# Band attention of a hybrid layer: projections handed out piece by piece between a head's steps, and fixed places for the values

## The chip, the cores and the metric

One core of a Trainium2 chip runs the whole kernel. The metric is the device time of one execution in microseconds (us). The profile is that of one execution; it reports times from the start of its span.

## The reference

The kernel computes one layer of an encoder on a sequence of 1024 frames with 1024 channels, in float32. A normalised and modulated input goes through one combined projection. Its columns feed two branches. Branch A is a gated DeltaNet with 8 heads. Branch B is band attention, and it is the part that the change is about: 16 heads of 64 channels, chunks of 64 frames, each chunk attending to itself and to the 8 chunks before it.

```python
def chunk_band_attention(q, k, v, rel_bias):
    ...
    bias = rel_bias.astype(jnp.float32)[:, idx]
    key_chunk = jnp.arange(band) // CHUNK
    scale = dh ** -0.5
    ...
```

For each head the scores are q·k times 0.125 plus a bias that depends on the distance; a softmax over the band follows, and then the product with the values. Each branch's output is projected to 1024 channels, both are multiplied with sigmoid gates and added, and a last projection, a residual, a layer norm and a feed-forward part follow.

## The kernel before

**Numbers in three parts.** Every large product is made from operands split in a high and a low part of type fp32r: high·high, high·low and low·high are summed in one PSUM bank. So a projection of 128 columns for 1024 frames takes 2 halves of 8 blocks of the inner dimension times 3 products, 48 matmuls of 128x512. `load_split` (L185) loads a block from DRAM and `split` makes its parts, the high one by ACT (L177) and the low one by DVE or POOL (L180).

**The band stage** (L870 to L1014) works in 8 pairs of heads. For a pair p it needs a block of queries (column block p) and one of keys (column block 8 + p), made by `qk_proj` and the code behind it, and values. The values come for four heads at once, from `v_proj` (L890 to L907): one group g serves pairs 2g and 2g + 1, and is 8 tiles of frames times 24 matmuls of 128x256, so 192 matmuls a group and 4 groups. Its results lie in four buffers, `vts[q][o]`, with q the pair and o the half of the frames.

**One head** (`attention`, L910 to L981) is four steps of 256 queries each; head 0 has six smaller ones. The chain of a step is:

- PE makes the scores `ps` (L933); DVE adds the bias and takes the minimum of the negated scores (L936, into `sb`, which lies in the places G and FT);
- ACT takes the exponential (L941), DVE the reciprocal of the sum (L943), POOL scales (L944);
- PE transposes in 128x128 pieces into `pp` (L959); ACT makes the high part `ph` (L962), DVE the low part `pl` (L963);
- PE multiplies with the values into `po` (L974); ACT and DVE add the two halves of the result (L979, L980) into `ob`.

A head takes 24 `ps` matmuls, 30 transposes and 36 `po` matmuls on PE; head 0 takes 52 `po`.

**Blocks made ahead.** Some blocks of queries and keys are not made beside their pair but earlier, and go through DRAM (`qk_d`): those in `EP` are made during the DeltaNet stage, those in `LP` by `late_qk_block` (L782) behind head 0. Numbers under 8 are queries, those from 8 on are keys. `qk_proj` then loads such a block into a staging buffer `raw` instead of multiplying. Before the change EP is (4, 12) and LP is (2, 14). For the two blocks of keys that come this way, half of the low parts `kl` are made by POOL (L1004), the others, and all for keys that come from PSUM, by DVE.

**After the attention** comes branch A's projection (L1020 to L1085): the eight blocks of `oa_d` are loaded and split into the place of the projections' input (`hh`, `hl`), so they can be split only when the last projection of queries or keys has read it. Then for j = 0 to 7 there are two halves of 24 matmuls `pbr` (L1047). Each half loads its gates from `gates_d` into a buffer `ma[j]` (L1051), and DVE multiplies gates and PSUM (L1053). The ring of banks for it has two entries, so a half can begin only when the half two before it has been multiplied with its gates.

**Places.** SBUF is a list of named places of 4 KB a partition. A buffer in a place that is still read waits for its last reader. Before the change the values are a ring over T0, T1, T2, T3, B5, B6 and are taken by four, so that group 3 lies in T0 to T3. The gates of branch A lie in `MA`:

```python
MA = (_E1[5], _E1[6], _E0[1], _E0[3], _E0[5], "GT", "SA", "SB")
```

Here `_E1[5]` is B5, `_E1[6]` is B6, and `_E0[i]` is Ai. In PSUM the projections have banks 0 and 1 (ring "qkv"), the scores 5, 6 and 2, the transposes 3 and 4, `po` bank 7, and branch A again 0 and 1.

**What sets the order.** The order on each engine is fixed when the program is built. The framework goes through the instructions by a priority that follows the order of the program text, and issues one when its operands and its buffers are there in its own plan; so work of a later line can come between the steps of an earlier one. On the chip, each engine then takes its instructions in that order and waits in it.

Of the kernel before, what the change touches and what calls it, by code (L numbers as in the profile page):

```python
# [2 lines left out]

# [41 lines left out]
PTR = 0  # L45
G0 = 1
GA = (3, 2, 2, 2, 3, 2, 2, 99)
EP = (4,12)
OL = (1,3,5)
EPP = 1  # L50
POM = 1
# [6 lines left out]
MS = 6  # L58
PWM = ()
PWL = 0  # L60
LP = (2,14)
TS = (0,1,2)
PL = (0,1,2,3)
XM = (0,2,4,6,7)
# [6 lines left out]
_T, _E0, _E1 = ([f"{n}{i}" for i in range(m)] for n, m in (("T", 4), ("A", 7), ("B", 7)))  # L71


def _at(group, step_, n, first=0):
# [24 lines left out]
    "v": (*_T, _E1[5], _E1[6]), "qs": (_E0[0], _E0[1], "GT"), "kh": (_E0[2], _E0[3], "SA"),  # L99
# [54 lines left out]
def hybrid_layer(  # L154
# [7 lines left out]
    PE, DVE, ACT, POOL, SP = nc.tensor, nc.vector, nc.scalar, nc.gpsimd, nc.sync  # L162
# [9 lines left out]
    def f(ap):  # L172
        return ap.bitcast(F32)
# [18 lines left out]
    w_ada2, w_in2 = w_ada[0], w_in[0]  # L192
# [37 lines left out]
    hh = hpool.tile([P, NK, S], F32R, tag="hh", name="hh")  # L230
# [638 lines left out]


    def qk_proj(c0, p):
        if (c0 - Q0) // P + p in EP + LP:
            raw = W.tile([P, S], F32, tag="raw", bufs=RB, name=nm("raw"))
            SP.dma_start(raw, qk_d[(c0 - Q0) // P + p])
            for n in range(2):
                yield slice(512 * n, 512 * n + 512), raw[:, 512 * n:512 * n + 512]
            return
        w = wblock(kview(w_in2, c0 + p * P, P), NK)
        halves = []
        for n in range(2):  # L880
            ps = pbank(nm("pqk"), "qkv")
            for k in range(NK):
                for a, r in ((w[0], hh), (w[0], hl), (w[1], hh)):
                    PE.matmul(ps, a[:, k, :], r[:, k, 512 * n:512 * n + 512],  # L884
                              start=(k == 0 and a is w[0] and r is hh),
                              stop=(k == NK - 1 and a is w[1]))
            yield slice(512 * n, 512 * n + 512), ps

    def v_proj(g):
        w = [wblock(w_in2[4 * P * i:4 * P * i + 4 * P,  # L890
                          Q0 + 2 * D + 256 * g:Q0 + 2 * D + 256 * g + 256].rearrange(
                              "(k p) n -> p k n", p=P), 4) for i in range(2)]
        vts = [[ring("v", [P, 4, 2, P], F32R) for _ in range(2)] for _ in range(2)]
        for t in range(NT):
            ps = pbank(nm("pv"), "qkv")
            for k in range(NK):
                wh, wl = w[k // 4]
                for r, a in ((hh, wh), (hh, wl), (hl, wh)):
                    PE.matmul(ps[:, 0:256], r[:, k, t * P:t * P + P], a[:, k % 4, :],  # L899
                              start=(k == 0 and r is hh and a is wh),  # L900
                              stop=(k == NK - 1 and r is hl))
            for q in range(2):
                dst = vts[q][t // 4][:, t % 4]
                src = ps[:, P * q:P * q + P].rearrange("p (e d) -> p e d", e=2)
                ACT.copy(dst[:, :, 0:64], src)
                DVE.tensor_tensor(dst[:, :, 64:P], src, f(dst[:, :, 0:64]), ALU.subtract)
        return vts  # L907


    def attention(h, qs_, khh, kll, vt_, ob):  # L910
        e = h % 2
# [7 lines left out]
        for ts in ((0, 1), (2, 3), (4,), (5,), (6,), (7,)) if z else ((0, 1), (2, 3), (4, 5), (6, 7)):  # L919
# [45 lines left out]
            for ji, j in enumerate(js):  # L965
# [6 lines left out]
                for pi in ((0, 1), (1, 0))[ji == len(js) - 1 and POM]:  # L972
# [6 lines left out]
            ACT.copy(tmp[a0:a0 + 64, :], po[b0:b0 + 64, 0:n])  # L979
            DVE.tensor_tensor(ob[a0:a0 + 64, P * t0:P * t0 + n], po[a0:a0 + 64, 0:n],  # L980
                              tmp[a0:a0 + 64, :], ALU.add)  # L981

    group("GA", "G", 4096)
    group("FA", "FT", 1024)
    group("X", _E1[4], 1024, F32R)
    vts = None
    for p in range(HB // 2):
        if p % 2 == 0:
            vts = v_proj(p // 2)
        qh = [ring("qs", [P, S], F32R) for _ in range(2)]  # L990
        kh_ = [ring("kh", [P, S], F32R) for _ in range(2)]
        kl_ = [ring("kl", [P, S], F32R) for _ in range(2)]
        for sl, ps in qk_proj(Q0, p):
            for e in range(2):
                a, b = (0, 64) if e == 0 else (64, 0)
                ACT.activation(qh[e][a:a + 64, sl], ps[a:a + 64, :], AF.Copy, scale=0.125)
                DVE.scalar_tensor_tensor(qh[e][b:b + 64, sl], ps[a:a + 64, :], 0.125,
                                         f(qh[e][a:a + 64, sl]), ALU.mult, ALU.subtract)
        for sl, ps in qk_proj(Q0 + D, p):
            for e in range(2):  # L1000
                E = slice(64 * e, 64 * e + 64)
                for d_ in (64 * e, 64 - 64 * e):
                    ACT.copy(kh_[e][d_:d_ + 64, sl], ps[E, :])
                    (POOL if p + NK in EP + LP and (EPP == 2 or EPP == 1 and d_ == 64 * e) else DVE).tensor_tensor(  # L1004
                        kl_[e][d_:d_ + 64, sl], ps[E, :], f(kh_[e][E, sl]), ALU.subtract)
# [636 lines left out]
```

## Time and profile before

| | us |
|---|---|
| median of 3 runs | 2214.96 |
| lowest and highest | 2212.79, 2216.69 |
| the profiled execution | 2214.56 |
| its span in the profile | 2212.5 |
| PE busy in the span | 2121.1 |
| DVE busy | 1551.0 |
| ACT busy | 1038.3 |
| POOL busy | 583.9 |

The profile gives, for each engine, busy time in stretches of the span ("windows"), in groups by source line, and the time that it waited with what ended the wait. PE is TensorE's stream of matmuls, PEld its loads of weights, which lie beside it; DVE is VectorE, ACT ScalarE, POOL GpSimd, and SP the engine that issues most DMAs. A matmul counts as busy while it is in the pipeline, so a busy PE can still be slower than PE at its best: how many matmuls of which size it got through in a stretch says more than its busy share. The column PEclk is the clock that TensorE was granted, 1.00 being full.

The band stage's matmuls lie between 840 and 1345 us of the span, beside the end of the DeltaNet stage in front and the first of branch A's products behind.

### The profile page before, as it was taken

What the parts mean: (1) busy time and instruction counts of PE and PEld (TensorE: products, weight loads), DVE (VectorE), ACT (ScalarE), POOL (GpSimd) and SP (SyncE); (2) the same over time, 40 slices, a digit from 0 to 9 for tenths busy, and PEclk for the clock granted to TensorE, in tenths of its full rate; (3) what the DMA queues carried; (4) which work ended last, traced back from release to release, by engine and by line L of the source; (5) the groups of instructions that cost most, each with busy time, mean ns of one, the idle gap of its engine ahead of it and who ended that gap; (6) DMA issues with size and microseconds to landing.
All of it is one profiled execution on the core that took longest, in us unless ns stands there. A gap on an engine that the chain in (4) does not pass through costs nothing.

```text
span 2212.5 us, 31630 instructions
## 1 busy us (share of the span) xinstructions
PE 2121.1 (96%) x11469; PEld 1773.4 (80%) x11469; DVE 1551.0 (70%) x3228; ACT 1038.3 (47%) x2216; POOL 583.9 (26%) x544
## 2 busy tenths in 40 slices
PE   6998999999999999999999899999899999999997
PEld 5787777888878787798989788888688888887876
DVE  8467475866767754567776653556998888889897
ACT  4645243434434334466675642235544444446453
POOL 4323222332223322223442422424011000000023
PEclk9999999999999999999999999999999999999999
DMA  9232323334232412211121424342243222263222
GB/s 287 76 106 80 101 89 110 103 94 119 75 112 75 143 35 97 70 51 51 61 66 61 149 93 136 105 152 87 67 155 102 85 83 81 76 218 134 96 94 87
DMA packets 228414, 224.67 MB, mean 102 GB/s; under 512 B 27482, under 2 KB 184595, under 8 KB 228259
## 3 DMA queue, kind: packets, MB, share of 16 engines
q1 hardware_dynamic: 217939, 218.96, 31.1%
q10 hardware_dynamic: 10320, 3.70, 0.7%
q8 instruction: 90, 1.47, 0.3%
q14 instruction: 65, 0.53, 0.1%
HBM read 180.63 MB, written 48.28 MB: 103 GB/s over the span
## 4 chain that ended last, share of the span: by engine, by line
PE 44%; DVE 5%; issue 1%; POOL 1%; ACT 1%; DMA 0%; DVEq 0%; SPq 0%; ACTq 0%; POOLq 0%
PE pup L1193 18%; PE pbr L1047 8%; PE pdn L1497 5%; PE pwo L1109 4%; PE pqk L884 2%; PE pv L899 2%; PE po L974 2%; PE pp L959 1%; PE ps L933 1%; DVE hl L180 1%; DVE hh L1585 1%; DVE hh L1511 0%; ACT hh L1580 0%; POOL hh L1555 0%; DMA raw<-in_w_branch_a_dram 0%
## 5 line engine op out<-in xcount | busy, mean ns | idle before, releaser
L180 POOL TENSOR_TENSOR wl<-raw,wh 128x1024 fp32r<-128x1024 f32 x88 | 211.1, 2401 | 307.1 <-ACT wh L177 298.2
L1193 PE MATMUL pup<-hh,wop 128*128 128x512 f32 x704 | 226.0, 392 | 1.9 <-DVE wop L180 1.0
L1193 PE MATMUL pup<-t,wop 128*128 128x512 f32 x792 | 189.8, 393 | 1.8 <-ACT t L177 1.8
L1193 PEld LDWEIGHTS pup<-t,wop 128*128 128x128 f32 x792 | 149.1, 188 | 35.5 <-ACT t L177 2.2
L177 ACT CAST wh<-raw 128x1024 fp32r<-128x1024 f32 x88 | 92.4, 1051 | 152.4 <-DMA raw<-in_w_in_dram 56.4
L1193 PEld LDWEIGHTS pup<-hh,wop 128*128 128x128 f32 x704 | 132.5, 188 | 31.4 <-DVE wop L180 1.5
L284 PE MATMUL pqkv<-hh,wh 128*128 128x512 f32 x352 | 142.8, 406 | 0.2 <-ACT GT L798 0.2
L1234 POOL TENSOR_TENSOR cc<-cc,G 128x512 f32<-128x512 f32 x22 | 41.0, 1864 | 379.5 <-DVE G L1216 325.4
L284 PE MATMUL pqkv<-hl,wh 128*128 128x512 f32 x352 | 139.9, 398 | 0.0
L284 PE MATMUL pqkv<-hh,wl 128*128 128x512 f32 x352 | 138.9, 396 | 0.0
L1193 PE MATMUL pup<-hl,wop 128*128 128x512 f32 x352 | 138.0, 392 | 0.4 <-DVE hl L180 0.4
L663 DVE TENSOR_TENSOR FT<-FT,G 128x16 f32<-128x16 f32 (+30 forms) x248 | 117.7, 475 | 16.5 <-POOL G L608 9.4
L944 POOL TENSOR_SCALAR G<-G,FT 128x640 f32<-128x640 f32 (+4 forms) x103 | 69.9, 681 | 191.3 <-DVE FT L943 169.6
L177 ACT CAST wop<-wr 128x512 fp32r<-128x512 f32 x110 | 66.5, 620 | 112.8 <-DVE wr L1179 64.5
L284 PE MATMUL pgt<-hh,wl 128*128 128x512 f32 x240 | 94.9, 396 | 0.8 <-POOL wl L180 0.8
L284 PE MATMUL pgt<-hl,wh 128*128 128x512 f32 x240 | 95.0, 396 | 0.0
L284 PE MATMUL pgt<-hh,wh 128*128 128x512 f32 x240 | 95.0, 396 | 0.0
L180 DVE TENSOR_TENSOR wop<-wr,wop 128x512 fp32r<-128x512 f32 x110 | 79.7, 730 | 19.1 <-ACT wop L177 18.6
L1497 PE MATMUL pdn<-hl 128*128 128x512 f32 x360 | 85.6, 391 | 2.3 <-ACT pdn L1492 1.5
L963 DVE TENSOR_TENSOR pl<-pp,ph 128x512 fp32r<-128x512 f32 (+2 forms) x116 | 72.5, 635 | 17.3 <-ACT ph L962 16.6
L1497 PEld LDWEIGHTS pdn<-hl 128*128 128x128 f32 x360 | 67.3, 188 | 17.8 <-ACT pdn L1492 1.9
L941 ACT ACTIVATE G<-G,FT 128x640 f32<-128x640 f32 (+4 forms) x103 | 71.6, 696 | 19.2 <-DVE FT L936 17.1
(457 smaller groups left out, 6113.4 us busy)
## 6 DMA issues: line engine op xcount, KB each, us to landing
raw<-in_w_in_dram SPq DMA_DIRECT2D x72, 512.0 KB
wr<-in_w_up_dram SPq DMA_DIRECT2D x44, 512.0 KB
raw<-in_w_ada_dram SPq DMA_DIRECT2D x32, 512.0 KB
dr<-g_d SPq DMA_DIRECT2D x18, 512.0 KB
dr<-in_w_down_dram SPq DMA_DIRECT2D x18, 512.0 KB
wa<-in_w_ada_dram SPq DMA_DIRECT2D x32, 256.0 KB
gates_d<-GT SPq DMA_DIRECT2D x32, 256.0 KB
g_d<-G SPq DMA_DIRECT2D x14, 512.0 KB
```

The lines of the kernel that those rows point to most:

```text
L177: ACT.copy(h, src)
L180: return le.tensor_tensor(l, src, f(h), ALU.subtract).ins
L284: PE.matmul(ps, a[:, k, :], r[k][:, 512 * n:512 * n + 512], start=(k == 0 and a is wh and r is rh), stop=(k == NK - 1 and a is wl))
L663: DVE.tensor_tensor(pr[:, :, 0:i + 1], ft[:, :, 0:i + 1], fa[:, i:i + 1, 0:i + 1].to_broadcast([P, 8, i + 1]), ALU.mult)
L884: PE.matmul(ps, a[:, k, :], r[:, k, 512 * n:512 * n + 512], start=(k == 0 and a is w[0] and r is hh), stop=(k == NK - 1 and a is w[1]))
L941: ACT.activation(sb[:, 0:n], sb[:, 0:n], AF.Exp, bias=mx[:, nb - 1:nb], scale=-1.0, accum_out=mx[:, 2:3])
L944: POOL.tensor_scalar(sb[:, 0:n], sb[:, 0:n], mx[:, 3:4], 0.0, ALU.mult, ALU.add)
L963: DVE.tensor_tensor(pl[:, B, :], pp, f(ph[:, B, :]), ALU.subtract)
L1047: PE.matmul(ps, a[:, k, :], r[k][:, N], start=(k == 0 and a is w[0] and r is rh), stop=(k == NK - 1 and a is w[1]))
L1109: PE.matmul(ps[n], a[:, t, k, :], wo[k][b][:, 512 * n:512 * n + 512], start=(k == 0 and a is mh and b == 0), stop=(k == NK - 1 and a is ml))
L1193: PE.matmul(ps, a[:, u, k, :], b[v][k], start=(new and k == 0 and u == 0 and v == 0), stop=(k == 3 and u == 1), skip_group_check=not new)
L1497: PE.matmul(sets[s_][i], a[:, u, i * P:i * P + P], b[:, v, :], start=(new and not seed and j == 0 and u == 0 and v == 0), stop=(j == len(q ...
```

## The change

It has four parts.

- **Pieces.** `attention`, `v_proj`, `late_qk_block` and the new `qk_pair` become generators that stop (`yield`) after a step, a tile of values, or half a block. `weave` runs one step of a head, then n pieces of other work, and what is left of it behind the last step.
- **What is beside what.** Beside each odd head lie the queries and keys of the next pair. Beside the even heads of pairs 0 to 6 lie, in this order: the two late blocks, value group 1 (two pieces a step), the halves of group 2, the halves of group 3, and late block 7. A half of group 2 or 3 is one half of the frames, so each half loads the group's weights again (`again`).
- **Blocks made ahead** are now queries only: EP is (4, 6), LP is (2, 5), and LQ adds block 7 beside head 12. Their number goes from 4 to 5. All low parts of keys are made by DVE.
- **Places of the values** are fixed by a table VS, by group, pair and half of the frames. The rows stand for groups 0 to 3. Group 3 lies in B6, T2 for pair 6 and T1, B5 for pair 7.

```diff
-EP = (4,12)
+EP = (4, 6)
-LP = (2,14)
+LP = (2, 5)
+LQ = {6: (7,)}
...
+VS = ((("T0", "T1"), ("T2", "T3")), (("B5", "T0"), ("B6", "T1")),
+      (("T2", "B5"), ("T3", "T0")), (("B6", "T2"), ("T1", "B5")))
...
     def attention(h, qs_, khh, kll, vt_, ob):
...
+            yield
...
-                    (POOL if p + NK in EP + LP and (EPP == 2 or EPP == 1 and d_ == 64 * e) else DVE).tensor_tensor(
-                        kl_[e][d_:d_ + 64, sl], ps[E, :], f(kh_[e][E, sl]), ALU.subtract)
+                    DVE.tensor_tensor(kl_[e][d_:d_ + 64, sl], ps[E, :], f(kh_[e][E, sl]), ALU.subtract)
+            yield
+
+    def weave(att, other, n):
+
+        for _ in att:
+            for _ in range(n):
+                next(other, None)
+        for _ in other:
+            pass
+
+    vg = [v_proj(g, g > 1) for g in range(HB // 4)]
+    for _ in chain(vg[0], qk_pair(0)):
+        pass
+    beside = {0: (chain(*map(late_qk_block, LP)), 1), 1: (vg[1], 2), 2: (islice(vg[2], 4), 1), 3: (vg[2], 1),
+              4: (islice(vg[3], 4), 1), 5: (vg[3], 1), **{p: (chain(*map(late_qk_block, i)), 1) for p, i in LQ.items()}}
     for p in range(HB // 2):
-        if p % 2 == 0:
-            vts = v_proj(p // 2)
...
         ob = ring("ob", [P, S])
         for e in range(2):
-            attention(2 * p + e, qh[e], kh_[e], kl_[e], vts[p % 2], ob)
-            if p == 0 and e == 0:
-                for q in LP:
-                    late_qk_block(q)
+            att = attention(2 * p + e, qk[p][0][e], qk[p][1][e], qk[p][2][e], vts[p // 2][p % 2], ob)
+            weave(att, *((qk_pair(p + 1) if p + 1 < HB // 2 else iter(()), 1) if e else beside.get(p, (iter(()), 1))))
```

The built orders of before and after are the same up to the first score of the band stage. They differ from there through branch A's products. Three places are shown.

On SP, near the end of the attention, before: the gates of branch A's first two blocks (`ma_12405` is j = 0, `ma_12406` is j = 1) among the loads of `oa_d`.

```order
L185 DMA raw_12433<-oa_d 128x1024 [waits DMAHW0_49,Pool_49]
L1051 DMA ma_12405<-gates_d 128x512 [waits PE_49]
L1051 DMA ma_12405<-gates_d 128x512
L1051 DMA ma_12406<-gates_d 128x512 [waits DMAHW2_49,PE_49]
L1051 DMA ma_12406<-gates_d 128x512 [waits DMAHW3_49]
L1012 DMA ob_d<-ob_10789 128x1024 [waits DMAHW4_49,DVE_49]
```

These gates stand ahead of the store of pair 5's output (the last row), so before heads 12 to 15 are done.

On SP at the corresponding place after (line 1077 is the old 1051): `ma_12436` is j = 0, and the last row is the store of the last pair's output.

```order
L1077 DMA ma_12443<-gates_d 128x512 [waits DMAHW3_49]
L1077 DMA ma_12443<-gates_d 128x512 [waits DMAHW4_49]
L1291 DMA B_1608_12433<-mod_d 16x128 [waits DMAHW5_49,PE_49]
L1077 DMA ma_12436<-gates_d 128x512 [waits DMAHW6_49,PE_49]
L1077 DMA ma_12436<-gates_d 128x512 [waits DMAHW7_49]
L190 DMA raw_12916<-ob_d 128x1024 [waits DMAHW0_49,DVE_49]
L1038 DMA ob_d<-ob_12054 128x1024 [waits DMAHW1_49,DVE_49]
```

The gates of j = 0 have moved from ahead of pair 5's store to the last rows before pair 7's. Place B5 holds the second half of pair 7's values, and the gates wait there for PE.

On PE, the end of the last head, before: `pbr_12790` belongs to branch A's j = 5.

```order
L1047 MATMUL pbr_12790<-hl,wh_12757 128x512
L1047 MATMUL pbr_12790<-hh,wl_12758 128x512
L1047 MATMUL pbr_12790<-hh,wh_12757 128x512
L974 MATMUL po_12385<-B_852_7310,v_11181 128x256 [waits Activation_49]
L1047 MATMUL pbr_12790<-hl,wh_12757 128x512
L1047 MATMUL pbr_12790<-hh,wl_12758 128x512
L974 MATMUL po_12385<-B_852_7310,v_11181 64x256 [waits DVE_49]
```

On PE at the same place after: `pbr_12554` belongs to j = 1, and line 1073 is the old 1047.

```order
L983 MATMUL po_12416<-ph_12395,v_10381 128x128
L983 MATMUL po_12416<-pl_12396,v_10381 64x128
L983 MATMUL po_12416<-pl_12396,v_10977 64x128
L983 MATMUL po_12416<-ph_12395,v_10977 128x128
L1073 MATMUL pbr_12554<-hh,wh_12548 128x512 [waits DVE_49]
L1073 MATMUL pbr_12554<-hl,wh_12548 128x512
L1073 MATMUL pbr_12554<-hh,wl_12549 128x512
```

Before, branch products stand between the rows of the last head, and five blocks of j and part of the sixth lie ahead of its end. After, the last head's rows stand alone, and j = 1 begins behind them. Counted over the whole order, from the last matmul of a query or key projection up to the last `po`: before 60 `ps`, 120 `po` and 270 `pbr`; after 76 `ps`, 144 `po` and 48 `pbr`. Those 48 are both halves of j = 0, and behind the last of them stand 46 `ps`, 104 `po` and 76 transposes with no other matmul among them.

On ACT, where pair 6's keys come in, before: `kh_11417` is made from the block that came through DRAM (`raw`).

```order
L962 CAST ph_10504<-pp_10513 128x384
L1003 CAST kh_11417<-raw_11485 64x512 x4
L1003 CAST kh_10650<-pqk_10756 64x512
L979 COPY G_7308<-po_10483 64x256
L941 ACTIVATE G_7308,FT_7309<-G_7308,FT_7309 128x640
```

After, the same pair's keys come from PSUM (`pqk`), line 1016 being the old 1003:

```order
L950 ACTIVATE G_7308,FT_7309<-G_7308,FT_7309 128x512
L1016 CAST kh_11284<-pqk_11402 64x512
L950 ACTIVATE G_7308,FT_7309<-G_7308,FT_7309 128x640
L1016 CAST kh_11284<-pqk_11402 64x512
L1016 CAST kh_11285<-pqk_11402 64x512 x2
```

The four copies stood in one row of four; they are now spread among the exponentials.

More of the change, by code (lines that the diff above doesn't have):

```diff
@@ L2 @@
 from contextlib import ExitStack, contextmanager, nullcontext
+from itertools import chain, islice
 import concourse.bass as bass
@@ L97 @@
        for i, n in enumerate(("egl", "kss", "rk", "bk", "bkk", "nbe", "eq", "so", "ro"))},
-    "v": (*_T, _E1[5], _E1[6]), "qs": (_E0[0], _E0[1], "GT"), "kh": (_E0[2], _E0[3], "SA"),
+    "qs": (_E0[0], _E0[1], "GT"), "kh": (_E0[2], _E0[3], "SA"),
     "kl": (_E0[4], _E0[5], "SB"), "ob": (_E0[6],), "ph": (_E1[0], _E1[2]), "pl": (_E1[1], _E1[3]), "ph0": ("GT",), "pl0": ("SB",),
@@ L871, in qk_proj @@
     def qk_proj(c0, p):
-        if (c0 - Q0) // P + p in EP + LP:
+        if (c0 - Q0) // P + p in EP + LP + sum(LQ.values(), ()):
             raw = W.tile([P, S], F32, tag="raw", bufs=RB, name=nm("raw"))
@@ L887, in qk_proj, with v_proj @@
             yield slice(512 * n, 512 * n + 512), ps
[L889 to L901, printed above, removed]
-            for q in range(2):
[L903 to L907, printed above, removed]
+    def v_proj(g, again):
+        for o in range(2):
+            if o == 0 or again:
+                w = [wblock(w_in2[4 * P * i:4 * P * i + 4 * P,
+                                  Q0 + 2 * D + 256 * g:Q0 + 2 * D + 256 * g + 256].rearrange(
+                                      "(k p) n -> p k n", p=P), 4) for i in range(2)]
+            for q in range(2):
+                vts[g][q].append(place(VS[g][q][o], [P, 4, 2, P], F32R, "v"))
+            for t in range(4 * o, 4 * o + 4):
+                ps = pbank(nm("pv"), "qkv")
+                for k in range(NK):
+                    wh, wl = w[k // 4]
+                    for r, a in ((hh, wh), (hh, wl), (hl, wh)):
+                        PE.matmul(ps[:, 0:256], r[:, k, t * P:t * P + P], a[:, k % 4, :],
+                                  start=(k == 0 and r is hh and a is wh),
+                                  stop=(k == NK - 1 and r is hl))
+                for q in range(2):
+                    dst = vts[g][q][o][:, t % 4]
+                    src = ps[:, P * q:P * q + P].rearrange("p (e d) -> p e d", e=2)
+                    ACT.copy(dst[:, :, 0:64], src)
+                    DVE.tensor_tensor(dst[:, :, 64:P], src, f(dst[:, :, 0:64]), ALU.subtract)
+                yield
@@ L981, in attention @@
                               tmp[a0:a0 + 64, :], ALU.add)
+            yield
     group("GA", "G", 4096)
@@ L985, in hybrid_layer, with qk_pair @@
     group("X", _E1[4], 1024, F32R)
-    vts = None
-    for p in range(HB // 2):
-        if p % 2 == 0:
-            vts = v_proj(p // 2)
+    vts = [[[], []] for _ in range(HB // 4)]
+    qk = {}
+    def qk_pair(p):
         qh = [ring("qs", [P, S], F32R) for _ in range(2)]
@@ L992, in hybrid_layer @@
         kl_ = [ring("kl", [P, S], F32R) for _ in range(2)]
+        qk[p] = qh, kh_, kl_
         for sl, ps in qk_proj(Q0, p):
@@ L998, in hybrid_layer @@
                                          f(qh[e][a:a + 64, sl]), ALU.mult, ALU.subtract)
+            yield
         for sl, ps in qk_proj(Q0 + D, p):
@@ L1003, in hybrid_layer @@
                     ACT.copy(kh_[e][d_:d_ + 64, sl], ps[E, :])
-                    (POOL if p + NK in EP + LP and (EPP == 2 or EPP == 1 and d_ == 64 * e) else DVE).tensor_tensor(
-                        kl_[e][d_:d_ + 64, sl], ps[E, :], f(kh_[e][E, sl]), ALU.subtract)
+                    DVE.tensor_tensor(kl_[e][d_:d_ + 64, sl], ps[E, :], f(kh_[e][E, sl]), ALU.subtract)
+            yield
+    def weave(att, other, n):
[9 more added lines that the diff above has]
+              4: (islice(vg[3], 4), 1), 5: (vg[3], 1), **{p: (chain(*map(late_qk_block, i)), 1) for p, i in LQ.items()}}
+    for p in range(HB // 2):
         ob = ring("ob", [P, S])
         for e in range(2):
-            attention(2 * p + e, qh[e], kh_[e], kl_[e], vts[p % 2], ob)
-            if p == 0 and e == 0:
-                for q in LP:
-                    late_qk_block(q)
+            att = attention(2 * p + e, qk[p][0][e], qk[p][1][e], qk[p][2][e], vts[p // 2][p % 2], ob)
+            weave(att, *((qk_pair(p + 1) if p + 1 < HB // 2 else iter(()), 1) if e else beside.get(p, (iter(()), 1))))
         SP.dma_start(ob_d[p], ob)
```

## The prediction

> **What bounds the kernel now.** The page's first part comes first: who is busy.
>
> ```profile
> span 2212.5 us, 31630 instructions
> PE 2121.1 (96%) x11469; PEld 1773.4 (80%) x11469; DVE 1551.0 (70%) x3228; ACT 1038.3 (47%) x2216; POOL 583.9 (26%) x544
> ```
>
> PE is the bound over the whole, and the change takes no matmul away. It can win only time in which PE runs below its pace. Next the windows of the band stage, all engines: PE, PEld, DVE, ACT, POOL, then granted clock, DMA share and GB/s.
>
> ```profile
> 925.40:1231.90 306.50, 296.48 (x2031) 271.81 (x2030) 215.47 (x650) 203.31 (x481) 108.48 (x139) 0.98 0.20 63
> 1044.00:1056.30 12.30, 10.82 (x71) 9.85 (x72) 9.80 (x35) 7.53 (x22) 4.18 (x7) 0.86 0.00 0
> 1143.40:1153.60 10.20, 9.31 (x68) 7.85 (x68) 8.34 (x31) 7.52 (x22) 2.54 (x4) 1.00 0.01 2
> 1231.90:1250.50 18.60, 12.26 (x69) 9.47 (x68) 16.18 (x43) 16.45 (x31) 12.87 (x9) 0.91 0.85 272
> 1231.90:1362.70 130.80, 124.46 (x655) 105.21 (x654) 64.50 (x156) 57.87 (x108) 45.25 (x35) 0.97 0.42 135
> 1260.00:1320.00 60.00, 60.00 (x336) 51.94 (x335) 31.07 (x89) 26.79 (x57) 18.73 (x17) 1.00 0.26 88
> ```
>
> I cut the stage in a middle (925.4 to 1231.9, where the last projection of queries or keys ends) and a tail (1231.9 to 1362.7, where branch A's last product ends). The 925 us in front I take as unchanged: the same first value group and first pair, and as many blocks made ahead there. In the second and third rows hardly any product stands between the steps (bare attention); in the last row branch A's products do, and PE is never idle. What PE waits for, from 840 to 1345 us, in total, times, longest:
>
> ```profile
> PE ps L933 <- DVE FT L936: 5.2, 9, 1.4
> PE pp L959 <- POOL G L944: 2.6, 3, 1.2
> PE pbr L1047 <- ACT wh L177: 2.4, 1, 2.4
> PE po L974 <- ACT B L962: 2.2, 3, 0.7
> ```
>
> These waits are short. DVE's minimum leads, and the loss is mostly bare steps at a slow pace, not one long stall.
>
> **Prices.** Three kinds of matmuls fill PE, so I want each one's pace with cover. First branch A's products (PE, PEld, clock, DMA):
>
> ```profile
> 1231.90:1250.50 18.60, 0.72 (x2) 0.55 (x3) 0.91 0.85 272
> 1260.00:1320.00 60.00, 45.97 (x188) 34.11 (x187) 1.00 0.26 88
> 1380.00:1440.00 60.00, 60.00 (x265) 49.45 (x264) 1.00 0.35 114
> ```
>
> Alone they take 60/265 = 0.2264 us each, and I give projections of queries and keys, of the same shape, the same. Then the scores (first fence) and the products with the values (second):
>
> ```profile
> 925.40:1231.90 306.50, 67.37 (x282) 45.13 (x283) 0.98 0.20 63
> 1044.00:1056.30 12.30, 4.22 (x16) 2.83 (x16) 0.86 0.00 0
> 1143.40:1153.60 10.20, 3.53 (x16) 2.39 (x16) 1.00 0.01 2
> 1231.90:1250.50 18.60, 5.39 (x22) 3.35 (x21) 0.91 0.85 272
> 1260.00:1320.00 60.00, 8.84 (x36) 6.06 (x36) 1.00 0.26 88
> ```
>
> ```profile
> 925.40:1231.90 306.50, 58.25 (x420) 52.62 (x420) 0.98 0.20 63
> 1044.00:1056.30 12.30, 4.84 (x32) 4.50 (x32) 0.86 0.00 0
> 1143.40:1153.60 10.20, 3.62 (x26) 2.82 (x25) 1.00 0.01 2
> 1231.90:1250.50 18.60, 4.03 (x24) 3.65 (x24) 0.91 0.85 272
> 1260.00:1320.00 60.00, 8.27 (x60) 7.68 (x60) 1.00 0.26 88
> ```
>
> A head has 24 scores and 36 value products; I count heads in a window as the mean of the two ratios. **Covered head:** in 1260 to 1320 the branch takes 188 x 0.2264 = 42.6 us, 17.4 are left for (36/24 + 60/36)/2 = 1.58 heads, so 11.0 us each. **Bare head:** 12.3 + 10.2 = 22.5 us for (32/24 + 58/36)/2 = 1.47 heads, 15.3 us each. DVE gives a second estimate; its four lines of a step (L936, L943, L963, L980) over all 16 heads:
>
> ```profile
> 840.00:1345.00 505.00, 96.21 (x384) 0.98 0.25 79
> 840.00:1345.00 505.00, 19.40 (x128) 0.98 0.25 79
> 840.00:1345.00 505.00, 83.88 (x146) 0.98 0.25 79
> 840.00:1345.00 505.00, 27.21 (x66) 0.98 0.25 79
> ```
>
> That is 226.7/16 = 14.17 us a head, more than PE's 11.0: bare, DVE is the bound. In the two bare windows it was busy 80% and 82%; 14.17/0.81 = 17.5. I take 16.4, between 15.3 and 17.5, so a bare head costs 5.4 us over a covered one; the bounds are 3.2 (DVE without a gap) and 6.5.
>
> **The middle: what it can win.** The projections of values (L899, first row the stage, second a stretch where PE did only these) and of queries and keys (L884):
>
> ```profile
> 925.40:1231.90 306.50, 84.84 (x576) 76.84 (x576) 0.98 0.20 63
> 1071.90:1074.90 3.00, 3.00 (x26) 3.00 (x26) 1.00 0.02 5
> ```
>
> ```profile
> 925.40:1231.90 306.50, 95.79 (x385) 70.30 (x384) 0.98 0.20 63
> ```
>
> At pace: 576 x 3.00/26 = 66.5, 384 x 0.2264 = 86.9, and (282/24 + 420/36)/2 = 11.7 heads x 11.0 = 128.7. Sum 282.1, so 24.4 us of the 306.5 are lost. More than that can't be won here.
>
> The change spreads 11.1 us of values (96 x 3.00/26) over an even head and a block or two of queries and keys (48 x 0.2264 = 10.9 each) over an odd one. What is late next is DVE. Its other operations:
>
> ```profile
> L1004 DVE TENSOR_TENSOR kl<-pqk,kh 64x512 fp32r<-64x512 f32 x48 | 33.0, 687 | 14.3 <-ACT kh L1003 13.7
> L997 DVE SCALAR_TENSOR_TENSOR qs<-pqk,qs 64x512 fp32r<-64x512 f32 x21 | 14.3, 688 | 5.8 <-ACT qs L996 5.3
> L906 DVE TENSOR_TENSOR v<-pv,v 128x128 fp32r<-128x128 f32 x48 | 13.3, 283 | 6.5 <-ACT v L905 6.2
> L1004 DVE TENSOR_TENSOR kl<-raw,kh 64x512 fp32r<-64x512 f32 x8 | 8.9, 1128 | 0.2
> ```
>
> In pairs 0 to 2 two blocks or a whole value group fill PE well past DVE's work. In pairs 3 to 6 PE has 2 x 11.0 + 10.9 + 11.1 = 44.0 us a pair, and DVE 2 x 14.17 + 8 x 0.687 + 4 x 0.688 + 8 x 0.283 = 38.9, so DVE must be busy 88% of the time. If it holds that, the pairs cost nothing more; if it only holds the 81% of the bare windows, a pair takes 48.0, 4.0 more, 14 us over some 3.5 pairs. I take 8, as cover lengthens the queue ahead of DVE but the chain of a step still runs through four engines, and 5 (2 to 7) for the edges of the early pairs, which no row shows. New loss 13, so the middle **wins 11.4**, between 3.4 (14 + 7 lost) and 19.4 (0 + 5).
>
> Moved loads: groups 2 and 3 load their weights twice, 4 more blocks to split. The splits' prices:
>
> ```profile
> L180 POOL TENSOR_TENSOR wl<-raw,wh 128x1024 fp32r<-128x1024 f32 x88 | 211.1, 2401 | 307.1 <-ACT wh L177 298.2
> L177 ACT CAST wh<-raw 128x1024 fp32r<-128x1024 f32 x88 | 92.4, 1051 | 152.4 <-DMA raw<-in_w_in_dram 56.4
> ```
>
> 4.2 us on ACT and 9.6 on POOL lie beside PE: ACT is idle 103 us and POOL 198 in the middle, and the DMA share is 0.20. I cost them at nothing; uncovered, one block late would be 3.5 us. The fifth block through DRAM is stored and loaded on SP in the same idle share. The `kl` parts that leave POOL and the DRAM copy cost DVE 16 x 0.687 = 11.0 where it had 9: nothing, except in the 88% above.
>
> **The tail: what it gives back.** Before, the tail's 130.8 us hold all 384 branch products (86.9 us; two of them in the row to 1250.5), and by the order 60 scores and 120 value products, 2.92 heads or 32.1 us. Lost: 11.8. After, only j = 0's 48 products lie in the attention, because its gates have to wait for place B5, that is for the last value product; both banks hold j = 0, and j = 1 queues behind the last head on PE. So:
>
> - behind j = 0 stand 46 scores and 104 value products, 2.40 heads bare: 2.40 x 5.4 = 13.0 (7.7 to 15.6);
> - in front of it, 30 and 40, or 1.18 heads, while `oa_d` is split. Before, the window 1231.9 to 1250.5 does this and loses 18.6 - 0.79 x 11.0 - 2 x 0.2264 = 9.4; the 0.39 head more costs 0.39 x 5.4 = 2.1. Sum 11.5 (9.4 to 14);
> - after the last `po`, j = 1 waits for the gates and the multiplication. The nearest row is branch B's first gates and multiplication:
>
> ```profile
> 1374.05 0.69 DVE L1055 SCALAR_TENSOR_TENSOR FT<-FT,pbr 128x512 f32<-128x512 f32 x1 [2.04 <-DMA FT<-gates_d]
> ```
>
>  2.04 + 0.69 and a short way to PE, 3.0 (2.7 to 5);
> - clock: the windows at 1044 and 1231.9 lost 12.3 x 0.14 and 18.6 x 0.09, 1.7 us each, in stretches with pauses no longer than the waits above. I add one such loss, 1.7 (0 to 3.4).
>
> [...]
>
> Sum 29.2, against 11.8: the tail **costs 17.4**, between 8 (7.7 + 9.4 + 2.7 + 0) and 26 (15.6 + 14 + 5 + 3.4).
>
> **Sum.** -11.4 + 17.4 = +6.0; the profiled execution's 2214.56, which is 0.4 under the median, becomes 2220.6. A measurement of this kernel can tell about 0.2%, 4.4 us, from no change.
>
> **The rivals.**
>
> 1. *DVE keeps up, faster.* It is busy 88% in pairs 3 to 6 and without a gap in bare heads: middle -19.4, tail +8, -11.4: 2203.2. For it: the longest waits of PE are 1.4 us on DVE, and cover absorbs such. Against: 80 to 82% where DVE was bound. It decides from a middle gain that is 4.4 above the tail's cost. Chance 0.28.
> 2. *They cancel.* For instance a full middle gain with the tail as I have it, -2.0: 2212.6. Chance 0.25.
> 3. *The pieces change little.* The framework put products between steps before, too; if the middle's 24.4 us are chain latency and not bare stretches, it wins 0 and the tail costs 17.4: 2232.0. For it: just two stretches in the windows are bare, 22.5 us, and at 15.3 - 11.0 they explain 1.47 x 4.3 = 6.3 of the 24.4. Against: the rest has to go somewhere, and even spacing hides chains. Chance 0.11.
>
> **How the numbers follow.** My forecast, the middle winning about 11 and the tail costing about 17, has 0.36 and a range of its own from 2219 to 2229. Slower is 0.36 + 0.11 = 0.47, the same 0.25, faster 0.28. The extremes of the terms are -19.4 + 8 and -3.4 + 26, 2203 to 2237; up to 2 in 10 lie outside 2203 to 2236, which is kept almost to the ends because the bare head's price rests on two short windows.
>
> **What would show it.** After: no PE window of the middle with over 5 us of bare attention; the middle's loss, worked out as above, at 13 (rival 1: 5; rival 3: 24); DVE over 85% busy in pairs 3 to 6 if it wins. In the tail: 48 branch products, then some 39 us with only attention, DVE over 80% and PE waiting for L936; then a gap of 3 us before j = 1, ended by DVE after the gates' DMA; and a granted clock under 1.0 there. I am wrong if branch products run between the steps of heads 14 and 15, if the bare heads take 12 us or less each, or if the middle wins nothing.

## The result and the profile after

The changed kernel takes 2226.34 us, the median of 6 runs (2221.46 to 2229.89), the kernel before 2213.83 (6 runs, 2210.49 to 2216.69). The ratio is 1.0055, with a 95% interval from 1.0043 to 1.0067: 12.2 us slower. The profiled execution took 2221.46, the shortest of the six, 6.9 more than that of before.

The page's first part, for the changed kernel:

```profile
span 2219.6 us, 31659 instructions
PE 2118.3 (95%) x11469; PEld 1767.3 (80%) x11469; DVE 1557.2 (70%) x3236; ACT 1047.0 (47%) x2222; POOL 580.5 (26%) x540
```

The matmuls are as many, and PE is busy 3 us less in a span 7 us longer. The windows of the changed kernel, all engines, show where: the middle (to the end of the last projection of queries or keys), the tail (to the end of branch A), and four pieces of the tail, which are the splits of `oa_d` beside j = 0, the bare heads, the gap, and the restart.

```profile
925.40:1216.90 291.50, 282.80 (x1953) 257.86 (x1951) 201.54 (x615) 194.45 (x458) 100.14 (x126) 1.00 0.20 63
1216.90:1371.90 155.00, 138.48 (x716) 115.84 (x716) 77.32 (x193) 69.84 (x136) 50.65 (x44) 0.96 0.41 133
1216.90:1249.30 32.40, 27.75 (x154) 23.46 (x154) 26.55 (x73) 26.14 (x51) 19.89 (x17) 0.89 0.58 188
1249.30:1290.50 41.20, 32.80 (x227) 28.00 (x225) 28.68 (x98) 29.69 (x70) 16.30 (x21) 0.96 0.40 135
1290.50:1294.00 3.50, 0.03 (x2) 0.02 (x1) 2.22 (x3) 0.36 (x1) 0.00 (x0) 0.98 0.65 176
1294.00:1298.00 4.00, 4.00 (x11) 3.20 (x12) 0.69 (x1) 0.97 (x1) 0.00 (x0) 0.59 0.94 336
```

Branch A ends at 1371.9 instead of 1362.7. The middle is 15.0 us shorter and the tail 24.2 longer, but the border between them has moved through the heads too, so both are set against their work at the prediction's prices. The rows of the scores (first two) and of the value products (last two):

```profile
925.40:1216.90 291.50, 60.36 (x266) 41.50 (x266) 1.00 0.20 63
1216.90:1371.90 155.00, 18.47 (x76) 12.19 (x76) 0.96 0.41 133
925.40:1216.90 291.50, 54.62 (x396) 49.02 (x396) 1.00 0.20 63
1216.90:1371.90 155.00, 22.17 (x144) 19.25 (x144) 0.96 0.41 133
```

The projections in the middle are L909 (values), L890 (queries and keys), and L289 (late block 7):

```profile
925.40:1216.90 291.50, 79.81 (x574) 72.25 (x572) 1.00 0.20 63
925.40:1216.90 291.50, 84.65 (x336) 61.38 (x336) 1.00 0.20 63
925.40:1216.90 291.50, 12.01 (x48) 8.76 (x48) 1.00 0.20 63
```

Middle: 291.5 - 574 x 0.1154 - 384 x 0.2264 - 11.04 heads x 11.0 = 16.9 us lost, against 24.4 before. Tail: 155.0 - 86.9 - 3.58 x 11.0 = 28.7, against 11.8. So by these two profiles the change wins 7.5 and gives back 16.9, +9.4, close to the 9.2 by which branch A ends later. The span grows by 7.1 only, as what follows branch A took 2.1 us less. What PE waited for from 1216.9 to 1298 us of the changed kernel, in total, times, longest:

```profile
PE pp L968 <- DVE pl L972: 4.6, 5, 2.7
PE po L983 <- DVE FT L945: 3.7, 2, 2.9
PE pbr L1073 <- DVE ma L1079: 3.5, 1, 3.5
```

The third row is the gap. The timeline around it, start and duration in us:

```profile
1290.55 1.00 SPq L1077 DMA_DIRECT2D ma<-gates_d  x2
1293.24 0.69 DVE L1079 SCALAR_TENSOR_TENSOR ma<-ma,pbr 128x512 f32<-128x512 f32 x1 [1.18 <-DMA ma<-gates_d]
1293.98 0.80 PE L1073 MATMUL pbr<-hh,wh 128*128 128x512 f32 x1 [3.47 <-DVE ma L1079]
```

The last value product started at 1290.25. Only then do the gates of j = 0 leave, land in place B5, and let DVE free the bank that j = 1 waits for. In the next 4 us PE's clock is 0.59.

### The profile page after: what moved, and what is told of

It is laid out like the page before. It is cut to its first block, busy times and chain, and to the rows that moved or that the text cites. A ratio compares the mean times of both kernels' runs of the same rounds, so it can differ in the third digit from the quotient of the medians.

```text
span 2219.6 us, 31659 instructions
## 1 busy us (share of the span) xinstructions
PE 2118.3 (95%) x11469; PEld 1767.3 (80%) x11469; DVE 1557.2 (70%) x3236; ACT 1047.0 (47%) x2222; POOL 580.5 (26%) x540
## 4 chain that ended last, share of the span: by engine, by line
PE 66%; DVE 18%; DMA 5%; issue 4%; ACT 3%; POOL 2%; SPq 1%; ACTq 0%; DVEq 0%; POOLq 0%
PE pup L1219 18%; PE pbr L1073 7%; PE pqkv L289 7%; PE pqk L890 5%; PE pwo L1135 4%; PE pv L909 4%; PE pgt L289 4%; DVE FT L668 3%; PE pdn L1523 3%; PE po L983 2%; DVE FT L670 2%; PE pp L968 2%; PE ps L942 2%; PE pz L289 2%; PE pqk L289 1%
## 5 line engine op out<-in xcount | busy, mean ns | idle before, releaser
L185 POOL TENSOR_TENSOR wl<-raw,wh 128x1024 fp32r<-128x1024 f32 x92 | 220.6, 2399 | 332.0 <-ACT wh L182 321.3
L289 PE MATMUL pqkv<-hh,wh 128*128 128x512 f32 x352 | 142.5, 405 | 0.2 <-ACT GT L804 0.2
L289 PE MATMUL pqkv<-hl,wh 128*128 128x512 f32 x352 | 139.7, 397 | 0.0
L289 PE MATMUL pqkv<-hh,wl 128*128 128x512 f32 x352 | 138.7, 396 | 0.0
L668 DVE TENSOR_TENSOR FT<-FT,G 128x16 f32<-128x16 f32 (+30 forms) x248 | 119.6, 482 | 17.4 <-POOL G L613 10.3
L289 PE MATMUL pgt<-hh,wl 128*128 128x512 f32 x240 | 94.9, 395 | 0.8 <-POOL wl L185 0.8
L289 PE MATMUL pgt<-hl,wh 128*128 128x512 f32 x240 | 95.0, 396 | 0.0
L289 PE MATMUL pgt<-hh,wh 128*128 128x512 f32 x240 | 95.0, 396 | 0.0
L1523 PEld LDWEIGHTS pdn<-hl 128*128 128x128 f32 x360 | 67.3, 188 | 17.2 <-ACT pdn L1518 1.9
L1279 DVE SCALAR_TENSOR_TENSOR G<-cc,vt,G 128x1023 f32<-128x1023 f32 (+1 forms) x58 | 74.2, 1280 | 8.2 <-ACT G L1276 8.1
```

The source lines that it names most:

```text
L185: return le.tensor_tensor(l, src, f(h), ALU.subtract).ins
L289: PE.matmul(ps, a[:, k, :], r[k][:, 512 * n:512 * n + 512], start=(k == 0 and a is wh and r is rh), stop=(k == NK - 1 and a is wl))
L668: DVE.tensor_tensor(pr[:, :, 0:i + 1], ft[:, :, 0:i + 1], fa[:, i:i + 1, 0:i + 1].to_broadcast([P, 8, i + 1]), ALU.mult)
L1279: DVE.scalar_tensor_tensor(y[:, d:], cc[:, :S - d], col("conv_f", tap * 44 + ti), y[:, d:], ALU.mult, ALU.add)
L1523: PE.matmul(sets[s_][i], a[:, u, i * P:i * P + P], b[:, v, :], start=(new and not seed and j == 0 and u == 0 and v == 0), stop=(j == len(q ...
```

## The experiments

In the table below, "lost" is what a stage took beyond its work at the prediction's prices, worked out from one profile of each kernel by its own windows as above (in e10 and e12 three products of branch B lie in the tail and count as work); the ratio is to the kernel before on the same chip, with its interval.

| kernel | ratio | middle lost | tail lost |
|---|---|---|---|
| before (e9: a second profile) | 0.9999 (0.9989 to 1.0009) | 24.4 (21.0) | 11.8 (13.3) |
| changed (e5: a second profile) | 1.0057 (1.0043 to 1.0071) | 16.9 (18.9) | 28.7 (29.2) |
| e1 changed, place free | 1.0031 (1.0018 to 1.0044) | | |
| e2 before, B5 in the ring | 1.0190 (1.0168 to 1.0212) | | 30.1 |
| e3 changed, unwoven | 1.0023 (1.0013 to 1.0033) | 15.0 | 25.8 |
| e4 before, queries ahead | 0.9997 (0.9986 to 1.0008) | 19.6 | 10.0 |
| e6 before, B5 by a table | 1.0064 (1.0051 to 1.0077) | 20.9 | 31.2 |
| e7 place free, weights first | 0.9984 (0.9974 to 0.9994) | 18.3 | 13.1 |
| e8 the same, unwoven | 0.9961 (0.9946 to 0.9976) | 15.7 | 9.5 |
| e10 woven at even heads | 0.9962 (0.9948 to 0.9977) | 18.1 | 10.4 |
| e11 woven at odd heads | 0.9968 (0.9957 to 0.9980) | 16.2 | 10.2 |
| e12 e8, all weights twice | 0.9988 (0.9978 to 0.9998) | 15.7 | 10.8 |

The theory at the start was the prediction's: the tail pays for place B5, and the middle gains from the pieces.

**The place (e1).** Branch A's gates get places in another order.

```diff
-MA = (_E1[5], _E1[6], _E0[1], _E0[3], _E0[5], "GT", "SA", "SB")
+MA = (_E0[1], _E0[3], _E0[5], _E1[6], "GT", "SA", "SB", _E1[5])
```

> The changed kernel with MA in another order: A1, A3, A5, B6, GT, SA, SB, B5, so that the gates of branch A's j = 0 go to a place that no value of pair 7 holds, and B5 comes last. Nothing else differs; in the built order 295 branch products stand between the last projection and the last value product, where the changed kernel has 48. Theory (the tail is paid for place B5): the tail's loss falls from 28.7 us to about the 11.8 of before, so some 17 us less than the changed kernel, about 2209, a ratio to before of 0.998 or less, and no wait of a branch product on DVE's multiplication over 1 us. Rival (heads 14 and 15 are slow for DVE, whatever PE has beside them, or the new loads cost the time): at most 4 us less, a ratio over 1.003.

Measured 2220.35 us, ratio 1.0031. That is 0.24% better than the changed kernel, 5 us, where 17 were expected. The rival had at most 4 and a ratio over 1.003, which the interval doesn't exclude. In the profile the bare heads have gone; other waits stand there instead. PE's waits of e1 from 1219 to 1380 us:

```profile
PE pbr L1073 <- ACT wh L182: 6.3, 2, 4.9
PE pp L968 <- DVE pl L972: 4.4, 2, 3.8
PE pbr L1073 <- DVE ma L1079: 2.2, 1, 2.2
```

The first row is not among the changed kernel's waits. The timeline of e1 at its end:

```profile
1343.13 0.34 SPq L1038 DMA_DIRECT2D ob_d<-ob  x1
...
1352.65 0.38 SPq L190 DMA_DIRECT2D raw<-in_w_branch_a_dram  x1
...
1356.85 1.04 ACT L182 CAST wh<-raw 128x1024 fp32r<-128x1024 f32 x1 [4.54 <-DMA raw<-in_w_branch_a_dram]
1357.95 0.80 PE L1073 MATMUL pbr<-hh,wh 128*128 128x512 f32 x1 [4.85 <-ACT wh L182]
```

The weights of j = 7 are asked for only at 1352.65. On SP they stand behind the gates of j = 7, which now have B5, behind loads of `ob_d` and behind the last pair's store. What SP waited for in e1, from 1330 to 1341 us (first row) and from 1345 to 1354 (the others):

```profile
SPq L1291 <- PE po L983: 5.0, 1, 5.0
SPq L190 <- DMA raw<-ob_d: 5.9, 1, 5.9
SPq L190 <- DVE ob L185: 2.3, 1, 2.3
```

The first wait is that of a small copy from `mod_d`, which waits for a value product; nothing behind it on SP leaves before it. The gates of j = 7 then leave at 1341.58, 0.3 us behind the start of the last value product, with no wait of their own on SP. The weights wait for something else: they need one of the three staging buffers `raw`, through which `ob_d` is loaded too, and get it when a block of `ob_d` has landed (5.9) and DVE has split it (2.3). So it was the loads of `ob_d` in front of them that made the weights late, and not, as e7's expectation has it, the wait for B5.

**The place alone, in the kernel before (e2).**

```diff
-    "v": (*_T, _E1[5], _E1[6]),
+    "v": (*_T[:3], _E1[5], _T[3], _E1[6]),
```

> The kernel before with one thing changed: the ring of the values is T0, T1, T2, B5, T3, B6, so that the second half of pair 7's values lies in B5, where the gates of branch A's j = 0 have to go. In the built order 48 branch products are left ahead of the last value product, where the kernel before has 270, and 36 scores and 84 value products, 1.92 heads, stand bare behind them. Theory: 1.92 bare heads at 5.4 to 7.6 us over a covered one, 10.4 to 14.6, then a gap of 3.5 and 1.9 for the clock, less the 2.4 of its loss that lay there before: 13 to 18 us slower than before, ratio 1.006 to 1.008. Rival (the changed kernel's loss is not of the place): under 4 us, ratio under 1.002.

Measured 2256.52, ratio 1.0190: 42 us, far more than either theory. The tail does what was expected: it is 149.1 us long (1249.4 to 1398.5) and loses 149.1 - 86.9 - 32.1 = 30.1, 18.3 more than before. The rest lies ahead of it. PE's waits of e2 from 780 to 925 us (first row) and from 925 to 1249 (second):

```profile
PE pvn L729 <- DVE vs L726: 5.0, 9, 0.7
PE pv L899 <- DVE kl L1004: 5.0, 2, 4.3
```

The ring of e2 put one of the four buffers of value group 0 into B5 as well, which the DeltaNet stage uses for `vs`; before, the wait of `pvn` was 0.5 us there. These two rows don't add up to what was lost ahead of the tail, and where the rest went stays open. So this edit was not the one meant, and e6 repeats it.

**The same by a table (e6).** Each `vts[q][o]` of before gets its place from a table, and groups 0 and 1 keep theirs.

```diff
-        vts = [[ring("v", [P, 4, 2, P], F32R) for _ in range(2)] for _ in range(2)]
+        vts = [[place(VS[g][q][o], [P, 4, 2, P], F32R, "v") for o in range(2)] for q in range(2)]
...
+VS = ((("T0", "T1"), ("T2", "T3")), (("B5", "B6"), ("T0", "T1")),
+      (("T3", "B5"), ("T2", "B6")), (("T0", "T1"), ("T3", "B5")))
```

> The kernel before with a table of places for the values in the place of the ring: groups 0 and 1 where they were, group 2 in T3, B5 and T2, B6, group 3 in T0, T1 and T3, B5. Unlike the ring with B5 fourth, group 0 stays out of B5, which the DeltaNet stage uses, so only the end of the attention should be touched. Theory (the gates' wait for B5): the tail loses 18 us more than before, as it did there, and the rest stays, ratio 1.007 to 1.009. Rival (the 42 us of the other ring were of something else than these two stages): ratio over 1.012 or under 1.003.

Measured 2228.98, ratio 1.0064. Here are the middle and the tail of e6:

```profile
925.40:1228.40 303.00, 292.51 (x2023) 266.98 (x2024) 215.30 (x650) 202.08 (x480) 108.31 (x139) 1.00 0.19 62
1228.40:1378.60 150.20, 134.46 (x656) 112.34 (x655) 65.63 (x156) 57.77 (x109) 45.43 (x35) 0.92 0.38 122
```

The tail holds as many matmuls as before's (x656 against x655), and takes 150.2 us instead of 130.8: 19.4 more. Nothing but the places of the last two value groups was changed, so the place costs the tail. The ratio's 14 us are less than that. Against the second profile of before (e9, below), the tail is 17.9 longer, the middle the same (303.0 and 303.3), and what follows branch A 2.7 us shorter; why the last is so is not shown. The expected 1.007 to 1.009 lies mostly above the interval.

**The pieces (e3).** In the changed kernel, `weave` runs each head whole, then the other work.

```diff
         for _ in att:
-            for _ in range(n):
-                next(other, None)
+            pass
         for _ in other:
             pass
```

> The changed kernel with the weaving undone alone: each head is written out whole, and the other work behind it, as the framework of before had it; places, blocks made ahead and the tail's wait for B5 stay. Theory (the pieces between the steps win the middle): the middle loses about 24 us again where the changed kernel loses 17, so some 7 us slower than the changed kernel, ratio to before about 1.009. Rival (the framework filled the steps before as well, and the middle's gain is that of blocks of queries instead of keys): within 2 us of the changed kernel, ratio 1.005 to 1.006.

Measured 2218.43, ratio 1.0023: 7 us faster than the changed kernel instead of 7 slower, so both theories missed it. The middle and the tail of e3:

```profile
925.40:1217.50 292.10, 287.33 (x1981) 263.96 (x1982) 209.72 (x633) 200.88 (x466) 100.93 (x128) 0.99 0.21 68
1217.50:1367.60 150.10, 135.50 (x698) 111.84 (x697) 74.60 (x181) 66.44 (x128) 49.84 (x43) 0.97 0.41 134
```

More matmuls (x1981 against x1953) lie in a middle of the same length. The theory that the pieces between the steps win the middle falls. The framework spreads other work between the steps anyway: in the traces, the longest bare run of the middle has 49 matmuls of scores, transposes and value products with the weaving, and 46 without.

**Queries ahead (e4).** The kernel before with EP and LP alone.

```diff
-EP = (4,12)
+EP = (4,6)
-LP = (2,14)
+LP = (2,5)
```

> The kernel before with EP (4, 6) and LP (2, 5) alone: the four blocks that go through DRAM are queries, all low parts of keys are made by DVE. Values, places and order of the text are as before; 247 branch products stand ahead of the last value product. Theory (weaving wins the middle): within 3 us of before, ratio 0.999 to 1.001. Rival (queries instead of keys win it): 7 us faster, ratio 0.997.

Measured 2213.61, ratio 0.9997: no difference, so e3's rival falls as well. What is left of the change is which other work belongs to which head: values in halves beside the even heads, the next pair beside the odd ones, in places that let the halves be filled early. This was not undone by itself, and neither was the fifth block made ahead. That these win the middle is argued from what was left over, and not shown.

**A second profile of each (e5, e9).** Both kernels unchanged.

> The changed kernel once more, on the same chip as the three beside it, since the unwoven one came out 0.3% faster than it on another chip. If the weaving costs something itself, the ratio to before is again 1.0055 and the unwoven kernel's 1.0023 lies clear of it; if the two differ by chip or by run, it is 1.002 to 1.004. A second profile shows whether the tail's 17 us and the middle's 7 hold from one execution to another, within 3 us each.

> The kernel before once more, for a second profile. By the prices of the prediction its middle lost 24.4 us in the first profile, at a granted clock of 0.98, but kernels with the same attention order lost 19.6 at 0.99 and 20.9 at 1.00. Theory (part of the 24.4 was that execution's clock): 19 to 22 us here, at 0.99 or 1.00. Rival (24 belongs to the kernel): 23.5 or more. The tail loses 10 to 12 either way.

The changed kernel gave 2227.20, ratio 1.0057, with 18.9 and 29.2 lost; before gave 2213.24, ratio 0.9999, with 21.0 and 13.3. So the tail's cost held (16.9 and 15.9), the middle's gain shrank from 7.5 to 2.1, and the weaving's loss against e3 is real (its interval is clear of e5's). The middle and the tail of e9:

```profile
925.40:1228.70 303.30, 293.13 (x2025) 268.34 (x2024) 215.44 (x650) 202.68 (x481) 108.50 (x139) 0.99 0.20 63
1228.70:1361.00 132.30, 126.91 (x656) 107.27 (x655) 64.38 (x156) 57.92 (x109) 45.22 (x35) 0.95 0.42 134
```

The middle took 303.3 at a granted clock of 0.99, where the prediction's profile had 306.5 at 0.98 for the same work. The trace shows where: in short stretches the clock is 0.50, and these are all that lie in the middles of before (two rows), e9 and e5; the middle of the first profile of the changed kernel has none (1.00).

```profile
1045.90:1049.30 3.40, 3.31 (x14) 3.27 (x15) 2.19 (x9) 1.83 (x6) 1.44 (x3) 0.50 0.00 0
1134.60:1141.40 6.80, 5.98 (x24) 5.52 (x25) 5.63 (x13) 4.49 (x11) 4.62 (x7) 0.50 0.17 48
1133.30:1136.70 3.40, 3.02 (x11) 2.86 (x12) 3.27 (x8) 3.35 (x10) 1.56 (x2) 0.51 0.30 96
939.80:943.20 3.40, 3.40 (x18) 3.40 (x17) 2.74 (x10) 2.18 (x7) 1.37 (x4) 0.50 0.00 0
```

With half of such a stretch taken as lost, an estimate from the 0.50 and 0.51 of these rows, the clock cost 5.1 us of before's middle, 1.7 of e9's, none of the changed kernel's and 1.7 of e5's. Without it the middle loses 19.3 in both profiles of before, and 16.9 and 17.2 in those of the changed kernel. So the middle's gain is about 2 us in both pairs, and the rest of the 7.5 was the clock of two executions. The tail's 13.3 is above the 10 to 12 expected.

**The place and the queue (e7), and unwoven (e8).** e1 with the loads of `ob_d` behind j = 7:

```diff
-                for k in {5: (0, 1), 6: (2, 3, 4), 7: (5, 6, 7)}.get(j, ()):
+                for k in {7: (0, 1, 2, 3, 4, 5, 6, 7)}.get(j, ()):
```

> The changed kernel with MA in the order A1, A3, A5, B6, GT, SA, SB, B5, and all eight loads of branch B's input (ob_d) put behind j = 7, so that the weights of branch A's j = 6 and 7 stand on SP ahead of the loads that wait for the end of the attention. Theory (with the place free, the loss moved to SP, where the last weights queue behind the wait for B5): the waits of 1.5 and 4.9 us and the slow clock behind them go, 8 us less than with the places alone, ratio about 0.9995. Rival (the splits of the eight blocks, now all at the end, are late for branch B): a wait of branch B's first products of 3 to 8 us comes, ratio 1.001 to 1.003.

> The same with each head written out whole and its other work behind it. With the middle's 7 to 9 us won by what stands beside which head, and not by the weaving, and the tail as before: ratio 0.996 to 0.998, faster than before and than the changed kernel. If the weaving is worth anything where the tail is clean, it is slower than the woven one by 2 us or more.

Measured 2209.13 (0.9984) and 2205.36 (0.9961). e7 is 0.47% under e1, 10 us, a little more than the 8 expected; the waits for `wh` are gone. e8 is the best kernel of the study: 8 us faster than before and some 20 faster than the changed kernel. Its middle and tail:

```profile
925.40:1219.80 294.40, 289.63 (x1996) 265.66 (x1995) 211.08 (x634) 202.34 (x469) 100.82 (x128) 0.99 0.22 68
1219.80:1353.60 133.80, 129.02 (x698) 109.95 (x697) 73.12 (x181) 65.45 (x126) 46.89 (x42) 0.97 0.45 146
```

e3's tail had the same 698 matmuls and took 150.1; with the place and the queue free it takes 133.8. So the two together are worth 16.3 us there, with the middle as it was.

**Where the weaving costs (e10, e11).** e7 with `next(other, None)` only for heads of one kind (`n if e == 0 else 0`, and `e == 1`).

> The kernel with the gates free and the weights first, woven beside the even heads (values, late blocks) alone; beside the odd heads the queries and keys stand behind the whole head. Woven everywhere it had a ratio to before of 0.9984, woven nowhere 0.9961. If the weaving's price lies at the odd heads, where 24 matmuls in one piece push between two steps and pair 7's keys are done half a head earlier, this one is at 0.996 to 0.997; if at the even heads, at 0.998 or more.

> The same woven beside the odd heads alone. If the price lies at the odd heads, 0.998 to 0.999; if at the even heads, 0.996 to 0.997; if half lies at each, this one and the other both at 0.997 to 0.998.

Measured 0.9962 and 0.9968. Neither half costs anything that these intervals tell from e8, while both together cost 0.2% (e7 against e8) to 0.3% (changed against e3). By the ratios none of the three expected cases fits; by the intervals half at each (0.997 to 0.998 for both) is not excluded. In the profiles e7 loses 2.6 us more than e8 in the middle and 3.6 more in the tail. A wait that the tails of e1 and e7 have and those of e8, e10 and e11 don't is a candidate. Here it is in e7, and below it a wait of e8 that takes 0.3 us in e7:

```profile
PE pbr L1073 <- DVE ma L1079: 2.3, 1, 2.3
PE ps L942 <- DVE FT L945: 3.2, 4, 1.8
```

In the first row a product of branch A waits for DVE to multiply an earlier half with its gates. As e8, e10 and e11 wait about as long for the second, the first is not shown to be the price; what the weaving costs stays open.

**The loads (e12).** e8 with `v_proj(g, True)` for all groups: four more blocks loaded and split, two of them beside head 2 and two in front of the band stage.

> The unwoven kernel with the gates free and the weights first, with the weights of value groups 0 and 1 loaded twice as well: 4 blocks more to load and split, as many as the change added. The prediction cost them at nothing, 3.5 us for each that comes late: ratio 0.996 as without them. Rival (a split on ACT and POOL is paid for among the steps): 4.2 us or more slower, 0.998 and over.

Measured 2210.24, ratio 0.9988: 6 us slower than e8. By the ratio the rival has it, but the place is another than it said. The middle, which holds half of the new loads, loses 15.7 in both. PE's waits of e12 from 780 to 925 us:

```profile
PE pzz L712 <- POOL SM L513: 3.9, 1, 3.9
PE pv L909 <- DVE v L916: 3.3, 1, 3.3
```

Neither row is among e8's there, whose longest wait is 1.6. The two blocks beside a head cost nothing, and the two in front about 6 us, presumably because PE has little else in its order there; the changed kernel loads twice only beside heads.

## Why the prediction was right, and where its terms were off

The forecast was slower, at 2220.6 for the profiled execution; that came at 2221.46. So close a hit is luck. That execution is the shortest of six; in it the tail cost what was forecast (16.9 against 17.4), the middle won 4 us less than forecast, and 2.1 us came back behind branch A, for which there was no term. Over all runs the change costs 12.2 us, twice the forecast 6.0; the median of 2226.34 lies inside the range to 2236. The direction and the tail's part of it are not luck.

- **The tail: right in cause and size.** Lost 28.7 and 29.2 in two profiles, forecast 29.2; e6 makes the same loss in the kernel before by the place alone, and e7 and e8, with the place and the queue free, take most of it away (13.1 and 9.5). By its terms: the 2.40 bare heads took 41.2 us, 17.2 each and 14.8 over covered ones (forecast 16.4, and 13.0). The first 1.18 heads with j = 0 lost 32.4 - 10.9 - 13.0 = 8.5, under the bound of 9.4; I had scaled a window in which just two branch products ran. The gap was 3.5 (forecast 3.0). The clock lost 4.0 x 0.41 = 1.6 at the restart (forecast 1.7). The clock was low where PE had no wait as long as the gap, too: the row from 1216.9 to 1249.3 is at 0.89, and no wait of PE in it was over 2.7.
- **Bare heads are DVE-bound: wrong as a reason, near as a price.** In the bare window DVE was busy 28.68 of 41.2 us, 70%, under the 80% that I expected to see. What it waited for there:

```profile
DVE FT L952 <- ACT G L950: 3.4, 3, 2.8
DVE ob L989 <- ACT G L988: 2.8, 3, 1.1
DVE pl L972 <- ACT ph L971: 2.4, 4, 1.4
```

DVE waits for ACT and PE for DVE: the chain of a step goes around, and no engine is full (PE, the busiest, was busy 32.80 of the 41.2 us). In the middle it is the same: from the store of pair 2 (1058.6) to the end of the middle DVE was busy 110.2 of 158.3 us, 70%, where the prediction had 88% of pairs 3 to 6 as needed.

- **The middle: right in sign, mis-sized.** Forecast 11.4, measured 7.5 in the first pair of profiles and 2.1 in the second pair, of the same two kernels; without the clock's part it is about 2 in both, below the low end of the forecast, 3.4. The term "new loss 13" was 17 without the clock's part, and the 24.4 that it was set against had 5.1 of the clock in it.
- **Its mechanism: wrong.** The step "the change spreads 11.1 us of values over an even head and a block or two over an odd one" gave the credit to the pieces. e3 and e8 lose less in the middle without them (15.0 and 15.7, against 16.9, 18.9 and 18.3), though each has two stretches of 3.4 us at half the clock in it. The sign that it named, no bare stretch of over 5 us in the middle, did not come: the trace of the changed kernel has six, the longest of 7.8 us. Before has seven, 58 us in all, and not just the two that the prediction counts. The third rival had half of this, that the framework put products between steps before, too; it did not have that the kernel wins in the middle without the weaving, which is put down here to the new neighbours by elimination.
- **The loads at nothing: held** beside heads (two blocks in e12's middle), on condition of the cover that the prediction named.
- **DVE keeps up (rival 1):** it did not come about; the middle's loss of 5 that it needed was never seen.

## What to carry to other kernels

When a buffer moves to a fixed place, look for the next user of that place in the order of every queue: here the first gates of the next stage waited for the last product of this one, which stopped the next stage on TensorE. When that was mended, the last weights were late behind loads that shared their staging buffers, on the same queue. Before weaving work by hand, undo only the weaving: a framework that issues by priority may already do it, and the gain may come from what was assigned to which place and head. A loss that is worked out from one profile carries that execution's clock; two profiles of the same kernel differed here by 3.2 us in a stage of 300, and the stretches at half the clock come to 3.4 of difference.

## What the runs showed of the hardware

The granted clock fell without a long wait of PE: it was 0.89 over 32.4 us of the changed kernel, where the longest wait was 2.7 us, and 0.86 over 12.3 us of before, where the longest was 1.4 (the wait of 2.4 in the prediction's list lies in another window, 1231.9 to 1250.5, at 0.91). Finer windows show what stands in front of it, in the changed kernel (first two rows) and in before:

```profile
1222.20:1225.60 3.40, 1.25 (x12) 1.11 (x10) 3.31 (x7) 3.35 (x9) 2.85 (x2) 1.00 0.79 245
1225.60:1232.40 6.80, 5.30 (x20) 4.28 (x21) 6.04 (x14) 6.68 (x14) 4.42 (x6) 0.50 0.63 189
1042.50:1045.90 3.40, 1.52 (x12) 1.14 (x10) 3.31 (x12) 2.36 (x8) 1.86 (x5) 1.00 0.00 0
```

In the middles and tails of these two profiles there are six stretches at 0.50, of 3.4 or 6.8 us, and in the 3.4 us in front of each PE was busy for 0.02 to 1.90 us. So some short waits close together went with as much loss of clock as one long one: in the changed kernel, 3.4 us at 0.50 stand from 1256.3, behind 3.4 us with PE busy for 1.22, and 3.4 us at 0.50 from 1293.9, behind the gap. Before's bare attention took 12.3 us at 0.86 for 0.78 heads, where the covered price is 8.6, and from 1143.4 on 10.2 us at 1.00 for 0.69 heads, where it is 7.6: the clock is part of the first loss and not of the second.
